# Differential attention on one core: the values as the stationary operand, four query tiles' probabilities moving, the result kept by feature

## The chip, the cores and the metric

The kernel runs on one core of one Trainium2 chip. The metric is the device time of one execution in microseconds. Before the change the median of three runs is 2161.65 us (2161.48 to 2164.58). The engines are TensorE (PE, whose weight loads are listed apart as PEld), VectorE (DVE), ScalarE (ACT), GpSimd (POOL) and SyncE (SP, which here only issues transfers). Each works through its own queue in order.

## The reference, cut to what matters

The program is one decoder layer: three branches (mLSTM, differential attention, cross-attention to a memory) from one normalised input h, merged with sigmoid gates, then an MLP. The change lies in the second branch. It has 8 heads, 1024 positions, query and key width 64 in two copies, and value width 128:

```
s = einsum('bhcqd,bhckd->bhcqk', qblk, kt) * scale      # c = 0, 1
s = where(kpos <= qpos, s, -inf)
p = softmax(s)
a = p[:, :, 0] - lam * p[:, :, 1]
o = einsum('bhqk,bhkv->bhqv', a, vt)
o = rms_norm(o, subln_g) * (1.0 - lam_init)             # over the 128 features of a head
```

Everything is float32. A product of matrices is made of three matmuls: each operand is split into a high part in the reduced format `F32R` and the rest (`split`: a cast on ACT, then a difference on DVE), and the terms high x high, high x low and low x high are summed in PSUM (`mm3`).

## The kernel before, in words

`branch_d` walks over 64 steps `s`, one for each head (`s // 8`) and each tile of 128 queries in it (`i8 = s % 8`). A head is thus two halves of four tiles; `hh` counts the 16 halves. In a step, `scores(s, 0)` and `scores(s, 1)` make the two score tiles (128 queries by up to 1024 keys, in PSUM), mask them and take the row maximum on DVE (L1029), and exponentiate on ACT with the row sum beside it (L1037). `combine(s)` weighs the second copy with lambda and the ratio of the sums and adds it to the first (L1046 to L1050, all on DVE). One step later `turn` transposes the combined probabilities in blocks of 128 by 128 on PE and splits them; two steps later `values` multiplies. There the turned probabilities are the stationary operand, and the values move: one matmul of 256 columns for (high, low) of the values and one of 128 columns for the probabilities' low part, for each block of keys. The two halves of the PSUM tile `po` are scaled by the first sum's reciprocal and added into `doS`, four tiles of queries by 128 features (L1088, L1089). After four steps, `norm` squares and sums over the features (L1098, L1100), takes the power -0.5 on POOL (`rsqrt_mean`, L148 and L149), multiplies (L1104), transposes the four tiles back to features by queries on PE, scales by the subln gain (L1110) and stores the half (`store_y`, L351). The tail of the program reads it much later.

Between these pieces `fill(n)` puts n steps of other matrix work on PE: first the generator `d_gemm`, which projects the query, key and value columns of the next heads (544 steps, the last 32 of them gate steps), then the generator `gates` (three matmuls of 512 columns a step). The gates that `fill` can still draw after those 544 are the 64 steps of the last two groups. While `self.pinned` is true, PE keeps exactly this order. On the other engines and the queue of SP a planner lays out the order when the program is built, and each works in that order.

`wino_gates` comes next: it makes the last gates with seven products for each eight. Its operands with numbers 0 to 2 lie in `hT`; numbers 3 to 6 are loaded from DRAM (`hx<-hc_d`, L1217, one megabyte each), and its weights come as `fr<-in_wgq` (L1188). Its products use, in this order, the operands 0, 2, 4, 5, 6, 3, 1. Its tiles lie in the memory that the tiles of `branch_d` give free: pools are laid one behind another in the order in which they are opened, from the end of the pool of weights `wpg`.

Of the kernel before, what the change touches and what calls it, by code (L numbers as in the profile page):

```python
# [17 lines left out]
P = 128  # L18
D = 1024
# [54 lines left out]
class Layer:  # L74
# [922 lines left out]
    def branch_d(self, pool, sums, gemm, kv, done):  # L997
# [3 lines left out]
        oS, info = {}, {}  # L1001
        gates = self.gates
        NS = 64

# [6 lines left out]
        def scores(s, c):  # L1011
# [4 lines left out]
            if c == 0:  # L1016
                info[s] = [
                    [pool.tile([P, D], F32, tag=f"dpe{q}", name=self.name("dpe")) for q in range(2)],
                    pool.tile([P, 8], F32, tag="dst", name=self.name("dst")),
                ]  # L1020
# [19 lines left out]
            )  # L1040

        def combine(s):
# [4 lines left out]
            V.scalar_tensor_tensor(  # L1047
                out=t8[:, 7:8], in0=t8[:, 7:8], scalar=t8[:, 4:5], in1=self.nlam, op0=ALU.mult, op1=ALU.mult
            )
            V.scalar_tensor_tensor(  # L1050
                out=pe[0][:, 0:n], in0=pe[1][:, 0:n], scalar=t8[:, 7:8], in1=pe[0][:, 0:n], op0=ALU.mult, op1=ALU.add
            )

        def turn(s, h2):

            hf, i = divmod(s % 8, 4)
            if h2 > hf:
                return
            nb = 4 if h2 < hf else i + 1
            pt = self.tp_tile()  # L1060
            for j in range(nb):
                c0 = (h2 * 4 + j) * P
                self.transpose(pt[:, j * P : (j + 1) * P], info[s][0][0][:, c0 : c0 + P])
            aT = pool.tile([P, 2, 512], F32R, tag="daT", name=self.name("daT"))
            self.split(aT[:, 0, 0 : nb * P], aT[:, 1, 0 : nb * P], pt[:, 0 : nb * P])
            info[s].append(aT)

        def values(s):
            hd, i8 = divmod(s, 8)
            hf, i = divmod(i8, 4)  # L1070
            t8 = info[s][1]
            po = self.po_tile()
            first = True
            for h2 in range(hf + 1):
                nb = 4 if h2 < hf else i + 1
                aT = info[s][2 + h2]
                v = kv[hd * 2 + h2][3]
                for j in range(nb):
                    s_ = slice(j * P, (j + 1) * P)
                    last = h2 == hf and j == nb - 1  # L1080
                    self.mm(po[:, 0:256], aT[:, 0, s_], v[j].rearrange("p a d -> p (a d)"), start=first, stop=False)
                    self.mm(po[:, 0:128], aT[:, 1, s_], v[j][:, 0], start=False, stop=last)
                    first = False
            if i == 0:
                oS[s // 4] = pool.tile([P, 4, P], F32, tag="doS", name=self.name("doS"))
            o = oS[s // 4]

            nc.scalar.activation(o[:, i], po[:, 0:128], AF.Copy, scale=t8[:, 6:7])  # L1088
            V.scalar_tensor_tensor(  # L1089
                out=o[:, i], in0=po[:, 128:256], scalar=t8[:, 6:7], in1=o[:, i], op0=ALU.mult, op1=ALU.add  # L1090
            )
            done[0] = s + 1

        def norm(hh, part):
            o = oS[hh]
            if part == 0:
                scr = pool.tile([P, 512], F32, tag="dscr2", name=self.name("dscr2"))
                nc.scalar.activation(scr, o.rearrange("p a d -> p (a d)"), AF.Square)  # L1098
                so = pool.tile([P, 4], F32, tag="dso", name=self.name("dso"))
                V.tensor_reduce(so, scr.rearrange("p (a d) -> p a d", a=4), axis=AX.X, op=ALU.add)  # L1100
                self.rsqrt_mean(so, so, 128, 4)
                info["so"] = so
            if part == 1:
                V.tensor_mul(o, o, info["so"].unsqueeze(2).broadcast_to([P, 4, P]))  # L1104
            if part == 2:
                pt = self.tp_tile()
                for i in range(4):
                    self.transpose(pt[:, i * P : (i + 1) * P], o[:, i])
                y = pool.tile([P, 512], F32, tag="y", name=self.name("yd"))
                nc.scalar.activation(y, pt, AF.Copy, scale=self.gsub)  # L1110
                self.store_y(1, hh // 2, hh % 2, y)
# [5 lines left out]
        for s in range(NS + 4):  # L1117
            hh, i = divmod(s - 2, 4)
            if s < NS:
                scores(s, 0)  # L1120
                fill(3)
            if 2 <= s < NS + 2:
                values(s - 2)
                if i == 3:
                    norm(hh, 0)
            fill(2 if s < NS else 6)
            if s >= 6 and i == 2:
                norm(hh - 1, 2)
            if s < NS:
                scores(s, 1)  # L1130
                fill(1)
            if s >= 6 and i == 1:
                norm(hh - 1, 1)
            if 1 <= s < NS + 1:
# [3 lines left out]
                if s == NS:  # L1138
                    fill(6)
# [829 lines left out]
```

## Time and profile before

| what | value |
|---|---|
| median of three runs | 2161.65 us |
| the profiled execution's own time | 2161.13 us |
| its span | 2159.3 us |
| granted TensorE clock | 1.00 |
| differential attention, first to last score | about 606 to 1080 us |
| its last values, last transposes | to 1097.7 and at 1112.6 us |
| last gates (`wino_gates`) | from 1113 us |

A row of a group of instructions gives line, engine, operation, written tile and read tiles, shapes and count; then busy time in all and mean nanoseconds of one; then the engine's idle time just before them and what ended it. The line L95 is that of the helper `mm`, L98 of `transpose`, L121 and L123 of `split`. The chain of waits lists pieces of the chain that ended last with start, length and count. Ends of matmuls are modelled, so their durations overlap; the spacing of their starts doesn't.

### The profile page before, as it was taken

Reading aid. Unit: us, or ns where it says so; the run is one execution under the profiler, and the core shown is the slowest. Engines: PE = TensorE matmul, PEld = TensorE weight load, DVE = VectorE, ACT = ScalarE, POOL = GpSimd, SP = SyncE. Lnnn points to the kernel's source line nnn. Section 1 sums busy time; section 2 is a strip of 40 time slices with the busy share of each in tenths; the row PEclk is TensorE's granted clock in tenths of the full one; section 3 lists DMA queues with packets and bytes.
Section 4 is the critical chain, followed back from the end, with each engine's and each line's share of the span. In section 5 each row is a group of like instructions: output and inputs, shape, how many; then the busy total and the mean of one; then the engine's idle time right before and its main releaser. Section 6 shows DMA issues by size and latency. Waiting matters only on the chain.

```text
span 2159.3 us, 30669 instructions
## 1 busy us (share of the span) xinstructions
PE 2133.7 (99%) x11049; PEld 1849.6 (86%) x11049; DVE 1421.0 (66%) x2688; ACT 987.2 (46%) x1991; POOL 578.5 (27%) x736
## 2 busy tenths in 40 slices
PE   7999999999999999999999999999999999999999
PEld 5888888898899999999878888888888888888887
DVE  6644475574548877777565433553688889876698
ACT  6543354454346666666554320223534544643331
POOL 2100000000111111111031003202756578565562
PEclk9999999999999999999999999999999999999999
DMA  6115122131433333333253643435434544844443
GB/s 240 46 61 171 39 86 75 41 93 47 171 89 94 98 98 84 92 84 83 79 175 132 237 157 109 147 97 195 160 131 153 201 151 156 295 169 151 156 161 107
DMA packets 134557, 275.95 MB, mean 128 GB/s; under 512 B 13025, under 2 KB 29702, under 8 KB 132358
## 3 DMA queue, kind: packets, MB, share of 16 engines
q1 hardware_dynamic: 128070, 254.07, 36.8%
q10 hardware_dynamic: 6336, 19.93, 2.4%
q8 instruction: 87, 1.43, 0.3%
q14 instruction: 64, 0.52, 0.1%
HBM read 177.45 MB, written 71.34 MB: 115 GB/s over the span
## 4 chain that ended last, share of the span: by engine, by line
PE 92%; DVE 2%; DMA 2%; ACT 1%; issue 0%; POOL 0%; SPq 0%; DVEq 0%; ACTq 0%; POOLq 0%
PE mm L95 52%; PE p L95 27%; PE sc L95 6%; PE po L95 3%; PE tp L98 3%; PE pr L98 1%; DMA hx<-hc_d 0%; PE tp L95 0%; DVE acc L69 0%; DVE w L123 0%; DMA ngb<-g_dng 0%; PE sc L98 0%; DMA wib<-g_dwi 0%; DVE u L69 0%; DMA raw<-in_wd 0%
## 5 line engine op out<-in xcount | busy, mean ns | idle before, releaser
L95 PE MATMUL mm<-w,hT 128*128 128x384 f32 (+3 forms) x2496 | 468.9, 331 | 0.9 <-DVE dsg L126 0.9
L95 PE MATMUL mm<-hT,w 128*128 128x512 f32 x1680 | 408.2, 394 | 0.6 <-ACT gt L500 0.6
L95 PEld LDWEIGHTS mm<-w,hT 128*128 128x128 f32 x2496 | 388.8, 189 | 11.0 <-DVE dsg L126 1.1
L95 PEld LDWEIGHTS mm<-hT,w 128*128 128x128 f32 x1680 | 308.3, 188 | 60.8 <-ACT gt L500 1.2
L95 PE MATMUL p<-xo,wo 128*128 128x512 f32 x1344 | 306.2, 390 | 0.4 <-DVE u L69 0.3
L95 PE MATMUL p<-xd,wo 128*128 128x512 f32 x1344 | 305.0, 390 | 0.0
L95 PEld LDWEIGHTS p<-xo,wo 128*128 128x128 f32 x1344 | 252.0, 188 | 53.3 <-DVE u L69 1.2
L95 PEld LDWEIGHTS p<-xd,wo 128*128 128x128 f32 x1344 | 252.3, 188 | 52.5 <-DVE acc L69 0.3
L95 PE MATMUL mm<-kt,w 128*128 128x512 f32 x1152 | 261.3, 390 | 0.0
L95 PEld LDWEIGHTS mm<-kt,w 128*128 128x128 f32 x1152 | 216.4, 188 | 44.8
L114 ACT CAST wo<-wraw 128x896 fp32r<-128x896 f32 x124 | 116.7, 945 | 223.0 <-PE p L95 86.6
L121 ACT CAST w<-raw 128x256 fp32r<-128x256 f32 (+3 forms) x272 | 139.5, 546 | 143.4 <-PE mm L95 123.2
L123 DVE TENSOR_TENSOR w<-raw,w 128x256 fp32r<-128x256 f32 (+3 forms) x272 | 158.3, 606 | 53.0 <-ACT w L121 52.3
L69 DVE TENSOR_TENSOR wo<-wraw,wo 128x896 fp32r<-128x896 f32 x124 | 151.6, 1232 | 46.5 <-ACT wo L114 46.5
L1288 POOL TENSOR_TENSOR wraw<-wraw 128x128 f32<-128x128 f32 x128 | 94.2, 736 | 214.5 <-DMA wraw<-in_wdown 74.6
L1037 ACT ACTIVATE dpe<-sc,dst,drr 128x256 f32<-128x256 f32 (+7 forms) x128 | 106.6, 833 | 96.7 <-DVE dst L1033 95.9
L148 POOL TENSOR_SCALAR hss<-hss 128x4 f32<-128x4 f32 x8 | 4.1, 516 | 408.7 <-ACT mscr L782 408.7
L1029 DVE CUSTOM_DVE_ANT_0 sc<-sc,tmask 128x256 f32<-128x256 f32 (+7 forms) x128 | 97.1, 759 | 13.8 <-PE sc L95 13.1
L1290 POOL TENSOR_TENSOR wraw<-wraw 128x128 f32<-128x128 f32 x128 | 96.7, 756 | 0.0
L95 PE MATMUL sc<-dk,dq 128*128 128x512 f32 (+3 forms) x384 | 92.0, 348 | 0.0
L1289 POOL TENSOR_TENSOR wraw<-wraw 128x128 f32<-128x128 f32 x128 | 90.5, 707 | 0.0
L69 DVE TENSOR_TENSOR acc<-acc,p 128x512 f32<-128x512 f32 x121 | 80.3, 685 | 15.0 <-PE p L95 14.4
(313 smaller groups left out, 3048.7 us busy)
## 6 DMA issues: line engine op xcount, KB each, us to landing
dk<-dsg SPq DMA_DIRECT2D x64, 256.0 KB, 4.3
wraw<-in_wup SPq DMA_DIRECT2D x64, 256.0 KB, 3.0
r_d<-xts SPq DMA_DIRECT2D x16, 1024.0 KB, 4.1
wraw<-in_wdown SPq DMA_DIRECT2D x64, 256.0 KB, 2.9
raw<-in_wd SPq DMA_DIRECT2D x32, 384.0 KB, 3.3
kraw<-y SPq DMA_DIRECT2D x24, 512.0 KB, 5.0
gl<-gates SPq DMA_DIRECT2D x48, 256.0 KB, 2.7
r_d<-rq ACTq DMA_DIRECT2D x16, 768.0 KB, 4.6
```

The source lines that it names most:

```text
L69: return self.tc.keep_in_program_order(f(*a, **k))
L95: self.pin(self.nc.tensor.matmul(out, l, r, start=start, stop=stop))
L98: self.pin(self.nc.tensor.transpose(out, x, self.ident))
L114: self.cast = self.A.copy(hi, src).ins
L121: a = nc.scalar.copy(hi, src)
L123: return a, nc.vector.tensor_sub(lo, src, f32(hi))
L148: g.tensor_scalar(r, ss, 1.0 / width, EPS, op0=ALU.mult, op1=ALU.add)
L1029: V.tensor_tensor_reduce(out=sc[:, 0:n], in0=sc[:, 0:n], in1=self.tmask[:, D - n : D], scale=1.0, scalar=-3.0e38, op0=ALU.add, op1=ALU.max ...
L1037: nc.scalar.activation(pe[c][:, 0:n], sc[:, 0:n], AF.Exp, bias=t8[:, 2 + c : 3 + c], scale=rr[:, i, c : c + 1], accum_out=t8[:, 4 + c : 5 ...
L1288: G.tensor_add(r[:, 4], r[:, 0], r[:, 3])
L1289: G.tensor_sub(r[:, 5], r[:, 4], r[:, 1])
L1290: G.tensor_sub(r[:, 6], r[:, 1], r[:, 0])
```

## The change

The values become the stationary operand, and the turned probabilities of four query tiles, up to 512 columns, move. So `turn(hh, j)` gathers block j of keys from the four query tiles of a half into one PSUM bank, and `values(hh, j)` makes three matmuls into `po`, which now holds features by queries. Key blocks on the diagonal use only the columns of the tiles that see them. The four combined tiles of a half have to stay until the last block is turned, so each has a buffer of its own, `pe0` to `pe7`. The division by the first sum can no longer be done on the result's rows: `combine` multiplies the second copy by its reciprocal and lambda on POOL, and DVE then multiplies the first copy by its own reciprocal and adds.

The result need not be transposed any more. Its sum of squares over the features runs over partitions: `squares` copies `po`, squares it and splits the squares, and `norm` multiplies them by a column of ones into one row of 512 sums. That row goes through DRAM to 128 partitions by 4, through `rsqrt_mean`, back to DRAM, and returns repeated on all partitions; one DVE instruction multiplies gain and root onto the copy.

The loop has slots, two a step: in slot n the block turned in slot n-1 is multiplied and the next one is turned. `T` gives the slot of each turn, `W` that of each norm. One bank `pt` and one bank `po` serve all turns and all values. After the 64 steps ten slots follow with `fill(4)` each, then `fill(8)` and the last norm. Buffers change: weights `w` 13 to 12, `dv` 17 to 16, `draw` 7 to 6, `doS` and `dpe0` go, `drt` and `pe0` to `pe7` come.

```diff
         def combine(s):
 ...
             V.reciprocal(t8[:, 6:8], t8[:, 4:6])
+            G.tensor_scalar(pe[1][:, 0:n], pe[1][:, 0:n], t8[:, 7:8], self.nlam, op0=ALU.mult, op1=ALU.mult)
             V.scalar_tensor_tensor(
-                out=t8[:, 7:8], in0=t8[:, 7:8], scalar=t8[:, 4:5], in1=self.nlam, op0=ALU.mult, op1=ALU.mult
+                out=pe[0][:, 0:n], in0=pe[0][:, 0:n], scalar=t8[:, 6:7], in1=pe[1][:, 0:n], op0=ALU.mult, op1=ALU.add
             )
 ...
+        def turn(hh, j, bank):
+            c = max(0, j - 4 * (hh % 2))
+            for i in range(c, 4):
+                self.transpose(bank[:, i * P : (i + 1) * P], info[hh * 4 + i][0][0][:, j * P : (j + 1) * P])
+            t = pool.tile([P, 2, 512], F32R, tag="daT", name=self.name("daT"))
+            c = slice(c * P, 512)
+            self.split(t[:, 0, c], t[:, 1, c], bank[:, c])
+            aT[hh, j] = t
+        def values(hh, j):
+            v, t = kv[hh // 2 * 2 + j // 4][3][j % 4], aT.pop((hh, j))
+            c = slice(max(0, j - 4 * (hh % 2)) * P, 512)
+            self.mm(po[:, c], v[:, 0], t[:, 0, c], start=j == 0, stop=False)
+            self.mm(po[:, c], v[:, 1], t[:, 0, c], start=False, stop=False)
+            self.mm(po[:, c], v[:, 0], t[:, 1, c], start=False, stop=j == hh % 2 * 4 + 3)
+        def squares(hh):
+            y = pool.tile([P, 512], F32, tag="y", name=self.name("yd"))
+            nc.scalar.copy(y, po)
+            sq = pool.tile([P, 2, 512], F32R, tag="daT", name=self.name("dsq"))
+            x = pool.tile([P, 512], F32, tag="dscr2", name=self.name("dscr2"))
+            nc.scalar.activation(x, po, AF.Square)
+            self.split(sq[:, 0], sq[:, 1], x)
+            Y[hh] = y, sq
+        def norm(hh, bank):
+            y, sq = Y.pop(hh)
+            for i in range(2):
+                self.mm(bank[0:1, :], ones[:, 0:1], sq[:, i], start=i == 0, stop=i == 1)
+            row = pool.tile([P, 512], F32, tag="drt", name=self.name("drow"))
+            nc.scalar.copy(row[0:1], bank[0:1, :])
+            so = pool.tile([P, 4], F32, tag="dso", name=self.name("dso"))
+            rt = pool.tile([P, 512], F32, tag="drt", name=self.name("drt"))
+            four = lambda d: d[hh].rearrange("(p i) -> p i", i=4)
+            Q = nc.sync
+            Q.dma_start(sums_d[hh : hh + 1], row[0:1])
+            Q.dma_start(so, four(sums_d))
+            self.rsqrt_mean(so, so, 128, 4)
+            Q.dma_start(four(root_d), so)
+            Q.dma_start(rt, root_d[hh].partition_broadcast(P))
+            V.scalar_tensor_tensor(out=y, in0=y, scalar=self.gsub, in1=rt, op0=ALU.mult, op1=ALU.mult)
+            self.store_y(1, hh // 2, hh % 2, y)
+        for hh in range(16):
+            for j in range(hh % 2 * 4 + 4):
+                T[8 * hh + 9 + (j if hh % 2 else 2 * j)] = hh, j
+        def slot(n):
+            bank = lambda: pt if n < 2 * NS else self.sc_tile()[:, 0:512]
+            if n - 1 in T:
+                hh, j = T[n - 1]
+                values(hh, j)
+                if j == hh % 2 * 4 + 3:
+                    squares(hh)
+                    W[n + 1] = hh
+            if n in W and W[n] % 2:
+                norm(W[n], bank())
+            if n in T:
+                turn(*T[n], bank())
+            if n in W and W[n] % 2 == 0:
+                norm(W[n], info["sc"][:, 512:] if n < 2 * NS else bank())
 ...
+        for s in range(NS):
+            scores(s, 0)
+            fill(3)
+            slot(2 * s)
+            fill(1)
+            scores(s, 1)
+            fill(3)
+            slot(2 * s + 1)
+            fill(1)
+            combine(s)
+        for n in range(2 * NS, 2 * NS + 10):
+            fill(4)
+            slot(n)
         fill(8)
-        norm(15, 2)
+        norm(15, self.sc_tile()[:, 0:512])
```

More of the change, by code (lines that the diff above doesn't have):

```diff
@@ L1040, in scores @@
             )
+            if c == 1:
+                done[0], info["sc"] = s + 1, sc
         def combine(s):
@@ L1054, in turn @@
[L1054 to L1111, printed above, removed]
+        def turn(hh, j, bank):
[6 more added lines that the diff above has]
+            aT[hh, j] = t
```

55 lines of the change are left out of this document (18 added, 37 removed).

## The prediction

> **What bounds the kernel now.** I read the profile's page, then busy time by stretches, then the chain of waits, then single groups. The page first:
>
> ```profile
> span 2159.3 us, 30669 instructions
> PE 2133.7 (99%) x11049; PEld 1849.6 (86%) x11049; DVE 1421.0 (66%) x2688; ACT 987.2 (46%) x1991; POOL 578.5 (27%) x736
> ...
> PE 92%; DVE 2%; DMA 2%; ACT 1%; issue 0%; POOL 0%; SPq 0%; DVEq 0%; ACTq 0%; POOLq 0%
> ```
>
> TensorE bounds it: 92% of the chain that ends last is PE. The stretches (columns: PE, PEld, DVE, ACT, POOL busy with counts, granted clock, DMA share, GB/s) show differential attention (620 to 1080), its end with the hand-over to the last gates, and those gates:
>
> ```profile
> 620.00:1080.00 460.00, 459.15 (x2902) 438.18 (x2901) 351.63 (x1028) 284.74 (x713) 64.63 (x60) 1.00 0.35 90
> 1080.00:1130.00 50.00, 47.68 (x233) 39.17 (x232) 31.50 (x50) 26.48 (x52) 16.26 (x21) 1.00 0.56 184
> 1130.00:1240.00 110.00, 110.00 (x485) 90.76 (x484) 57.55 (x86) 41.72 (x68) 11.49 (x15) 1.00 0.52 180
> ```
>
> In the body PE lacks 0.85 us of 460 and DVE has 24% left, so there a saved microsecond of matmul is a saved microsecond. In the 50 us of the hand-over PE is idle 2.3 us already: that place is thin.
>
> **What a matmul really costs.** The busy durations of matmuls overlap, so I price by the chain of waits (start, length, count):
>
> ```profile
> 836.80 1.56 PE mm L95 x9
> 838.36 1.33 PE po L95 x12
> 843.20 0.33 PE tp L98 x3
> 1091.34 0.44 PE tp L98 x4
> 1091.78 4.13 PE mm L95 x18
> 1095.91 1.79 PE po L95 x16
> 343.50 1.08 PE sc L95 x9
> ```
>
> 384 columns cost 1.56/9 = 0.173 us, 512 columns (the gates' mm) 4.13/18 = 0.229, 258 columns (the sc at 343.50) 0.120, and a transpose of 128 columns 0.110. A po pair, 256 and then 128 columns, costs 1.33/6 = 0.222 or 1.79/8 = 0.224: 0.103 for the narrow one, nearly twice its share of 0.120. A stationary block of 128 columns thus has a floor of about 0.11.
>
> The Trainium skill (TensorE: Matmul & The Clock Gate, LDWEIGHTS) puts a weight load at columns / 1.2 ns, 107 ns for 128: the trace agrees. Its rule in Back-to-back issue gap, columns / 2.4 + 2.5 ns, would leave a narrow matmul at 56 ns and speaks against this change; the sum by it stands among the rivals, and the trace disagrees with it.
>
> **The change on PE.** Counts and shapes now:
>
> ```profile
> L95 PE MATMUL po<-dv,daT 128*128 128x256 f32 x288 | 69.5, 321 | 0.0
> L95 PE MATMUL po<-dv,daT 128*128 128x128 f32 x288 | 64.1, 223 | 0.1
> L98 PE MATMUL tp<-ident,dpe 128*128 128x128 f32 x288 | 47.0, 272 | 0.0
> L98 PE MATMUL tp<-ident,doS 128*128 128x128 f32 x64 | 9.6, 272 | 0.0
> ```
>
> Removed: 288 pairs x 0.223 = 64.2, and the 64 transposes of the result x 0.110 = 7.0. Added: per head the even half has value steps of 512, 384, 256 and 128 columns, the odd half five of 512 and then 384, 256, 128; with three matmuls each that is 18 x 0.229 + 6 x 0.173 + 6 x 0.120 + 6 x 0.110 = 6.54 us, x 8 heads = 52.3. The sum over features by the column of ones: 16 x 2 matmuls of 512 columns = 32 x 0.229 = 7.3. The 288 transposes of probabilities stay. Net 52.3 + 7.3 - 64.2 - 7.0 = **-11.6 us**; with 0.222 to 0.224 per pair, -11.3 to -11.9.
>
> **The other engines in the body.** Per half of a head (16 of them), from these rows:
>
> ```profile
> L1047 DVE SCALAR_TENSOR_TENSOR dst<-dst,dv 128x1 f32<-128x1 f32 x64 | 13.9, 217 | 1.2
> L1089 DVE SCALAR_TENSOR_TENSOR doS<-po,dst,doS 128x128 f32<-128x128 f32 x64 | 22.4, 350 | 45.5 <-ACT doS L1088 45.5
> L1100 DVE TENSOR_REDUCE dso<-dscr 128x4 f32<-128x512 f32 x16 | 11.0, 684 | 7.0 <-ACT dscr L1098 7.0
> L1104 DVE TENSOR_TENSOR doS<-doS,dso 128x512 f32<-128x512 f32 x16 | 11.5, 721 | 6.6 <-POOL dso L149 6.6
> L123 DVE TENSOR_TENSOR dsg<-pr,dsg 128x512 fp32r<-128x512 f32 x16 | 11.0, 688 | 2.3 <-ACT dsg L121 2.2
> L1050 DVE SCALAR_TENSOR_TENSOR dpe<-dpe,dst,dpe 128x512 f32<-128x512 f32 x8 | 6.0, 750 | 0.2
> L1098 ACT ACTIVATE dscr<-doS 128x512 f32<-128x512 f32 x16 | 10.1, 632 | 6.7 <-DVE doS L1089 6.7
> L121 ACT CAST daT<-tp 128x512 fp32r<-128x512 f32 x48 | 27.5, 586 | 18.0 <-PE tp L98 17.5 <-PE mm L95 0.4
> ```
>
> DVE loses 4 x (0.217 + 0.350) + 0.684 + 0.721 = 3.67 and gains one split (0.69) and one product (0.75), so it falls by 2.2 x 16 = 36 of 352 us. ACT trades four evictions, a square and the scaled copy for a copy, a square, a cast and the row's copy: about even. Neither gates PE, so I credit nothing.
>
> New is a POOL instruction in every combine: DVE's product now waits for it. No row has its shape; the nearest ones:
>
> ```profile
> L1871 POOL MEMSET tmask<- 128x1024 f32 x1 | 0.9, 949 | 0.0
> L1162 POOL TENSOR_TENSOR hb<-hb,hb 128x512 f32<-128x512 f32 x4 | 6.0, 1502 | 20.2 <-DVE hb L1161 8.8 <-DVE hb L1157 7.4 <-PE tp L98 4.0
> L149 POOL TENSOR_TENSOR drr<-drr,mhalf 128x16 f32<-128x16 f32 x16 | 46.4, 2901 | 1.3
> SPq L351 <- ACT yd L1110: 77.7, 7, 11.3
> ```
>
> With no tensor read, 1024 columns take 0.95; with two, 3.0 (twice the 512 row). Over the mean width of 576 that is 0.53 to 1.7 us, 64 times. Queued on DVE behind the waiting product are the next mask-and-maximum and the splits of turned probabilities, for which PE waits one slot later. But a tile is now first turned two slots, a whole step of some 7 us, after its second scores at the earliest, and were DVE to stand for all of 64 x 1.7 = 109 us, 352 - 36 + 109 = 425 of the remaining 449 us still fit. POOL's 2.9 us power can delay 16 of the 64. I take 1 us of PE stalls, bounds 0 and 6. The norm's relay through DRAM (four dependent transfers on SP per half) blocks the loads behind it; SP stands as long in this trace (up to 11.3 us for the y store) with PE at 99.8%, and the y it makes is read only in the tail: nothing. The smaller rings (w 12, draw 6, dv 16) release their slot before it is asked for again: nothing either.
>
> **The end.** Here I expect the loss.
>
> ```profile
> 1097.55 15.21 PE L95 MATMUL mm<-hT,w 128*128 128x512 f32 x66
> 1112.60 0.60 PE L98 MATMUL tp<-ident,doS 128*128 128x128 f32 x4
> 1116.55 3.06 PE L95 MATMUL mm<-hT,w 128*128 128x512 f32 x12 [0.60 <-ACT gt L500]
> 1129.46 3.06 PE L95 MATMUL mm<-hx,w 128*128 128x512 f32 x12 [1.58 <-DVE u L1248]
> 1079.44 0.99 SPq L1217 DMA_DIRECT2D hx<-hc_d  x2
> 1085.01 1.05 ACT L121 CAST hx<-hx 128x1024 fp32r<-128x1024 f32 x1 [1.61 <-DMA hx<-hc_d]
> 1086.09 1.23 DVE L123 TENSOR_TENSOR hx<-hx 128x1024 fp32r<-128x1024 f32 x1 [0.85 <-ACT hx L121]
> 1087.56 1.05 ACT L121 CAST hx<-hx 128x1024 fp32r<-128x1024 f32 x1 [0.30 <-DMA hx<-hc_d]
> SPq L351 <- ACT yd L1110: 10.2, 1, 10.2
> ```
>
> Now 66 gate matmuls, 15.2 us, stand between the last value matmul and the last transposes; they hide the norm and the loads of the next operands. The fills are 544 of the projection's steps and then 64 gate steps. The new loop has spent 572 when scores end and asks for 4 before each of ten tail slots: 36 are left, so slots 128 to 136 get theirs, and slot 137 and the closing fill(8) get nothing. PE then waits three times, in program order. (1) For the split of the last turned tile: 0.27 transpose, 0.27 and 0.28 for cast and difference of 128 columns, hand-overs: 1.0 us. (2) For copy, square, cast and difference before the ones: 0.59 + 0.63 + 0.59 + 0.69 and 0.3 of hand-overs = 2.8. (3) For operand 4 of the gates. Behind their common base the new pools lie as 6 + 8 + 18 KB, then three daT buffers of 4; the gates' as 4 + 16 + 16 KB and then operand 4, at 36 to 52 KB, on the second and third daT. With 4 + 96 + 16 tiles in that ring the last squares sit in the second, so the load starts after the ones matmuls. Two such loads asked for together at 1079.44 were cast from 1085.01 and 1087.56: 5.6 and 8.1 us; with 1.05, 1.23 and 0.3 that is 8.2 to 10.7, against 24 matmuls of cover, 5.5. So 2.7 to 5.2; I take 3.5, near the undisturbed load. Together 7.3, less the 2.3 idle there now: **+5.0**; bounds +1.5 (no third wait) and +12 (two more casts ahead in ACT, a late load).
>
> **Sum.** -11.6 + 1 + 5.0 = -5.6 us. The profiled execution took 2161.1 (its span of 2159.3 and 1.8 around it), 0.5 below the median of 2161.65: 2155.5 by it, 2156.1 by the median. I say **2156**.
>
> **Rivals.**
> A hidden end: the planner gets the operands loaded early and other work covers the norm. The end costs +1.5 or less and the body 0 to 1: 2150. For it: fr2 now lies on buffers that are free early. Against: nothing is left on PE between.
> Stalls in the body: POOL's product at 3.0 us for deep tiles, behind the 2.9 us power, eats what is left, 64 x 0.08 = 5 us more: 2161. For it: DVE's in-order queue. Against: the 24% that DVE has free.
> The relay ahead of the load (slower): SP issues in order, and the 10.2 us stand behind a y store shows what it does to the gates' loads. If the last norm's first three transfers and the power stand ahead of operand 4, three hops of 2.4 to 3.5 and 1.2 us make the third wait 8 to 12 longer: 2161.1 - 11.6 + 1 + 5 + 11 = 2167. It decides from about two hops.
> Narrow matmuls at their streaming rate alone (slower): with 0.060 for 128 columns, half of 0.120, the values go from 288 x 0.180 = 51.8 to 49.9, the transposes removed are worth 3.8 and the ones cost 7.3: +1.6, and with the body's 1 and the end's 5 it is 2169. Sixteen po matmuls in 1.79 us deny it, where 8 x 0.18 would be 1.44.
>
> The Trainium skill's gap rule is this last rival: by its 216, 162, 109 and 56 ns the sum is 46.8 + 6.9 - 47.6 - 3.6.
>
> **Chances.** Forecast (2152 to 2160) 0.46, hidden end 0.19, body stalls 0.16, relay 0.15, streaming rate 0.04. About 0.2%, 4.3 us, is what can be told from no change: faster is below 2157.3, that is two thirds of the forecast and the hidden end, 0.50; slower is above 2166, most of the relay and the last, 0.16; the same 0.34. The range, 2149 to 2167, leaves out the last case and half of the relay's upper part.
>
> **What would show it.** The three value forms at about 0.23, 0.17 and 0.12 us in the chain and PE at 99.5% or more in the body show the first term; PE idle there with DVE named as releaser, and DVE waiting for POOL in combine, the second. In the last 30 us before the gates PE should stand near 1, 2.8 and 3.5 us, released by the split, by the squares' split and by hx. A body that isn't some 11 us shorter makes the prediction wrong, and so does an end without idle PE.

## The result and the profile after

The changed kernel takes 2230.31 us (median of 4 runs, 2228.8 to 2231.61) beside 2161.57 us for the kernel before on the same chip: a ratio of 1.0315, interval 1.0299 to 1.033. It is 68.7 us slower, where 2156 us and at most 2167 us were predicted. The profiled execution took 2229.75 us, its span 2228.0.

First the page of the changed kernel: its span, the busy time of the engines, and the shares of the chain that ended last.

```profile
span 2228.0 us, 29966 instructions
PE 2142.7 (96%) x10729; PEld 1830.1 (82%) x10729; DVE 1392.3 (62%) x2561; ACT 974.8 (44%) x1959; POOL 647.8 (29%) x800
...
PE 45%; DMA 6%; DVE 5%; POOL 4%; issue 4%; ACT 3%; SPq 1%; ACTq 0%; DVEq 0%; POOLq 0%
```

TensorE (PE) has dropped from 99% of the span to 96%, and from 92% of the chain to 45%. The rest of the chain runs through the other engines and through DMAs: the kernel is no longer bound by its matmuls alone. The count of matmuls is as the change says, 11049 - 576 - 64 + 288 + 32 = 10729.

Next, busy time by stretches (columns as in the prediction: PE, PEld, DVE, ACT, POOL, clock, DMA share, GB/s), first after, then the same end stretch before.

```profile
620.00:1080.00 460.00, 423.54 (x2410) 385.80 (x2409) 303.12 (x847) 248.42 (x634) 120.93 (x115) 0.99 0.36 93
1080.00:1210.00 130.00, 105.50 (x471) 84.65 (x470) 63.87 (x119) 56.63 (x114) 29.00 (x35) 0.92 0.36 110
```

```profile
1080.00:1210.00 130.00, 127.68 (x585) 105.07 (x584) 78.67 (x123) 64.12 (x117) 27.75 (x35) 1.00 0.54 185
```

In the body PE now lacks 36.5 us of 460 where it lacked 0.85; in the 130 us of the end it lacks 24.5 us where it lacked 2.3. VectorE (DVE) is busy for 303 us of the body where it was 352, so it is not short of time.

For an account of the whole span I price each matmul by its columns (0.4167 ns a column and 14 ns, at least 110 ns; this fits the prediction's 0.110, 0.173 and 0.229) and call excess what lies between the starts of two consecutive matmuls above that price. Over the span the priced work falls from 2122.8 to 2108.8 us, by 14.0, and the excess rises from 24.8 to 107.6, by 82.8. That is +68.8, the change of the span. Because the stages shift, I divide the excess by stage: the body goes from 600 us to the start of the last score (1079.0 us before, 1118.5 after), the end from there to 1215. In the body the excess rises from 4.2 to 60.4 us, at the end from 3.4 to 26.4, elsewhere by 4. Body and end excess below are meant so.

Who waits for whom between 600 and 1240, by the view of waits (total, times, longest):

```profile
DVE dpe L1059 <- POOL dpe L1058: 48.0, 45, 2.7
POOL dso L148 <- DMA dso<-d_ss: 37.5, 10, 9.6
DVE yd L1107 <- DMA drt<-d_rs: 34.2, 16, 5.0
PE mm L95 <- ACT u L1246: 16.2, 1, 16.2
PE tp L95 <- DVE daT L123: 14.2, 14, 1.8
PE tp L95 <- ACT daT L121: 8.7, 14, 1.4
PE sc L95 <- ACT dpe L1046: 8.0, 7, 1.7
```

The first three are waits of VectorE and GpSimd (POOL), 120 us together, that the kernel before did not have. The last four are PE's own. (The value matmuls are named tp here, since `po` now comes from `tp_tile`.)

Three kinds of stall come back from head to head. (A) The product of a finished half with its root stands in VectorE's queue, waiting for the last hop of the relay through DRAM, and the split of the next turned probabilities stands behind it. From the timeline (start, length, engine, instruction, idle time before it and releaser):

```profile
819.29 0.57 ACT L121 CAST daT<-tp 128x512 fp32r<-128x512 f32 x1
820.55 0.63 PE L95 MATMUL tp<-daT,dv 128*128 128x512 f32 x2
821.56 0.75 DVE L1107 SCALAR_TENSOR_TENSOR yd<-yd,dv,drt 128x512 f32<-128x512 f32 x1 [2.97 <-DMA drt<-d_rs]
822.23 0.68 DVE L123 TENSOR_TENSOR daT<-tp,daT 128x512 fp32r<-128x512 f32 x1
822.97 0.50 PE L95 MATMUL tp<-daT,dv 128*128 128x512 f32 x1 [1.80 <-DVE daT L123]
```

ACT had cast that tile by 819.86; VectorE stood 2.97 us for `drt`, then took the product and the split, and PE stood 1.80 us ahead of the third value matmul. (B) The combine. VectorE waits for GpSimd's scale, and GpSimd, in this instance, for the relay's sums:

```profile
813.78 0.17 DVE L1057 RECIPROCAL dst<-dst 128x2 f32<-128x2 f32 x1 [0.78 <-ACT dpe L1046]
814.31 0.20 POOL L148 TENSOR_SCALAR dso<-dso 128x4 f32<-128x4 f32 x1 [3.97 <-DMA dso<-d_ss]
814.59 1.01 POOL L149 TENSOR_TENSOR dso<-dso,mhalf 128x4 f32<-128x4 f32 x1
815.60 0.55 POOL L1058 TENSOR_SCALAR dpe<-dpe,dst,dv 128x256 f32<-128x256 f32 x1
816.18 0.49 DVE L1059 SCALAR_TENSOR_TENSOR dpe<-dpe,dst,dpe 128x256 f32<-128x256 f32 x1 [2.24 <-POOL dpe L1058]
```

The scale, 0.55 us of work, starts 1.65 us after its factor was ready at 813.95. (C) The ones matmuls of the even halves wait for ACT's exponential, because they write into the upper bank of the score tile whose lower columns ACT is reading: 8.0 us in 7 waits above.

At the end the predicted three waits are all there:

```profile
1156.86 0.65 PE L95 MATMUL tp<-daT,dv 128*128 128x128 f32 x3 [0.47 <-ACT daT L121]
1159.97 0.40 PE L95 MATMUL sc<-dsq,dso 128*1 128x512 f32 x1 [2.46 <-ACT dsq L121]
1160.70 0.40 PE L95 MATMUL sc<-dsq,dso 128*1 128x512 f32 x1 [0.33 <-DVE dsq L123]
1161.91 0.25 SPq L1102 DMA_DIRECT2D d_ss<-drow  x1
1165.99 0.34 SPq L1103 DMA_DIRECT2D dso<-d_ss  x1
1169.60 1.88 POOL L149 TENSOR_TENSOR dso<-dso,mhalf 128x4 f32<-128x4 f32 x1
1171.51 0.34 SPq L1105 DMA_DIRECT2D d_rs<-dso  x1
1172.92 0.34 SPq L1106 DMA_DIRECT2D drt<-d_rs  x1
1173.31 0.43 SPq L1222 DMA_DIRECT2D hx<-hc_d  x1
1181.90 1.99 ACT L121 CAST hx<-hx 128x1024 fp32r<-128x1024 f32 x2 [10.00 <-DMA hx<-hc_d]
1184.43 2.08 PE L95 MATMUL mm<-hx,w 128*128 128x512 f32 x4 [16.24 <-ACT u L1246]
```

The first is 0.47 us, the second 2.46 + 0.33, the third 16.24: the last load of the gates' operands (L1222) is issued only at 1173.31, behind the four transfers of the last norm on SyncE's queue and the root on GpSimd between them. From its issue to its cast on ACT it takes 8.6 us more.

### The profile page after: what moved, and what is told of

Its sections match the earlier page's. It is cut to its first block, busy times and chain, and to the rows that moved or that the text cites. A ratio compares the mean times of both kernels' runs of the same rounds, so it can differ in the third digit from the quotient of the medians.

```text
span 2228.0 us, 29966 instructions
## 1 busy us (share of the span) xinstructions
PE 2142.7 (96%) x10729; PEld 1830.1 (82%) x10729; DVE 1392.3 (62%) x2561; ACT 974.8 (44%) x1959; POOL 647.8 (29%) x800
## 4 chain that ended last, share of the span: by engine, by line
PE 45%; DMA 6%; DVE 5%; POOL 4%; issue 4%; ACT 3%; SPq 1%; ACTq 0%; DVEq 0%; POOLq 0%
PE p L95 22%; PE mm L95 21%; DMA drt<-d_rs 2%; ACT dpe L1046 1%; POOL dpe L1058 1%; DMA dso<-d_ss 1%; POOL dso L149 1%; PE tp L95 1%; DVE dpe L1059 1%; POOL drr L149 1%; DMA wraw<-in_wdown 1%; DMA d_rs<-dso 1%; DVE u L69 1%; DVE sc L1038 0%; PE sc L95 0%
## 5 line engine op out<-in xcount | busy, mean ns | idle before, releaser
L95 PE MATMUL mm<-w,hT 128*128 128x384 f32 (+3 forms) x2496 | 459.8, 330 | 2.2 <-DVE dst L1042 1.6
L95 PEld LDWEIGHTS mm<-w,hT 128*128 128x128 f32 x2496 | 394.3, 190 | 15.0 <-issue 2.9
L95 PEld LDWEIGHTS p<-xd,wo 128*128 128x128 f32 x1344 | 251.7, 188 | 56.2 <-DVE c L69 1.9
L1058 POOL TENSOR_SCALAR dpe<-dpe,dst,dv 128x128 f32<-128x128 f32 (+3 forms) x64 | 56.8, 888 | 286.0 <-DVE dst L1057 249.5
L95 PE MATMUL tp<-daT,dv 128*128 128x512 f32 (+3 forms) x288 | 74.9, 357 | 23.1 <-DVE daT L123 14.2
```

The lines of the kernel that those rows point to most:

```text
L95: self.pin(self.nc.tensor.matmul(out, l, r, start=start, stop=stop))
L1058: G.tensor_scalar(pe[1][:, 0:n], pe[1][:, 0:n], t8[:, 7:8], self.nlam, op0=ALU.mult, op1=ALU.mult)
```

## Experiments

All times stand beside runs of the kernel before on the same chip. Its medians lay between 2162.6 and 2164.1, so I compare ratios to it; 0.001 is 2.2 us. The changed kernel has 1.0315.

### Taking the suspects away

e1_no_relay: the relay goes, and the root with it.

```
-            (so, rt, four DMAs, rsqrt_mean)
-            V.scalar_tensor_tensor(out=y, in0=y, scalar=self.gsub, in1=rt, ...)
+            V.scalar_tensor_tensor(out=y, in0=y, scalar=self.gsub, in1=y, ...)
```

> Leaves out the root of the norm: the row of sums is made and copied out as before, but its four transfers through DRAM and the two POOL instructions go, and the last product multiplies the copy by the gain and by itself. Theory 'relay': the DVE product that waits for the returning row (34 us of standing in the changed kernel, 16 times) and the POOL pair that waits for the row's sums (37 us, with combine's scaling behind it) hold up the splits that PE waits for, and the last operand load of the gates is queued on SP behind the last relay. Then some 20 to 30 us go in the body and 11 to 14 at the end: 2230 becomes 2187 to 2200, and DVE has no row that waits for a transfer of the norm. Theory 'POOL': combine's scaling on POOL is what holds DVE up; then only the end moves, 2216 to 2220, and PE in the body still lacks some 35 us of 460.

e2_scale_on_dve: the combine's scale moves.

```
-            G.tensor_scalar(pe[1][:, 0:n], ...)
+            V.tensor_scalar(pe[1][:, 0:n], ...)
```

> Same computation; combine's scaling of the second copy moves from POOL to DVE, so that DVE waits for no other engine between the row sums and the combined tile. Theory 'POOL': DVE stood 48 us in 45 waits for that instruction, most of it in front of work PE waits for; without it 2195 to 2208. Theory 'relay': DVE only exchanges a wait for work of 0.3 to 1.1 us each, 64 times; 2222 to 2232.

e3_neither has both edits.

> Both of the last two edits; leaves out the root of the norm. If relay and POOL together make the body's stalls, PE in the body lacks no more than 10 us of what it lacked 36 of, the end keeps a wait for the last squares and a short one for the operand, and the time is 2160 to 2172. If the order of the slots itself (one PSUM bank for all turns, the ones matmuls one slot after the squares) makes them, it stays above 2180.

e4_tail_cover: two filling products instead of four between the tail's slots, which keeps more of them for the end.

```
-            fill(4)
+            fill(2)
             slot(n)
```

> Same computation; only the ten tail slots draw 2 instead of 4 gate steps each, so 16 of the 64 gate steps, 11 us of matmuls, are left to run behind the last values and the last norm. If PE's 16 us wait before the first product with a loaded operand comes from having nothing to do while the relay and the load run, it falls by 9 to 11, less 2 to 4 for thinner tail slots: 2221 to 2226. If the slots in the tail are bound by their splits, it is given back there: 2228 to 2232.

Measured: e1 2203.48 us (1.0186, 1.0171 to 1.0201), e2 2203.37 (1.0187, 1.017 to 1.0204), e3 2192.47 (1.0138, 1.0123 to 1.0153), e4 2225.44 (1.0286, 1.0271 to 1.0301). The body of each, e1, e2, e3:

```profile
620.00:1080.00 460.00, 426.65 (x2442) 392.48 (x2441) 310.26 (x860) 257.02 (x644) 104.14 (x94) 0.99 0.34 88
```

```profile
620.00:1080.00 460.00, 441.89 (x2534) 405.37 (x2533) 349.73 (x950) 265.61 (x668) 69.34 (x62) 1.00 0.38 98
```

```profile
620.00:1080.00 460.00, 436.87 (x2494) 404.49 (x2493) 344.85 (x939) 264.07 (x660) 49.97 (x34) 0.98 0.35 90
```

Without the relay the excess falls from 26.4 to 13.0 us at the end and from 60.4 to 49.2 in the body, so e1 lies between its two cases. It also shows that the relay is not what makes VectorE wait for the scale, for that wait is as long without it:

```profile
DVE dpe L1059 <- POOL dpe L1058: 49.0, 47, 2.6
```

With the scale on VectorE (e2, within its first band) the gain lies in the body, 60.4 to 32.5, although VectorE is then busier by 47 us; so it was not VectorE's load that cost. The two gains do not add up: 28 us each and 38 together. e3 is above 2180, as its second case said. What is left in it is the third kind of stall, which has grown:

```profile
PE sc L95 <- ACT dpe L1046: 18.8, 7, 3.0
```

```profile
673.67 0.68 DVE L123 TENSOR_TENSOR dsq<-dscr,dsq 128x512 fp32r<-128x512 f32 x1
675.19 0.46 ACT L1046 ACTIVATE dpe<-sc,dst,drr 128x128 f32<-128x128 f32 x1
675.80 1.01 PE L95 MATMUL sc<-dsq,dso 128*1 128x512 f32 x2 [2.85 <-ACT dpe L1046]
```

The squares were split by 674.35; the ones matmuls started at 675.80, after the exponential of the score tile whose bank they borrow. Seven waits of 2.7 us on the average, in seven of the eight heads. e4's time is within its band, 6 us less, but not by what was expected: the third wait of the end falls from 16.2 to 13.7 us only, by 2.5 instead of 9 to 11. More cover helps little.

### The borrowed bank

e5_late_ones: the even halves' ones matmuls come one slot later, when the tile kept in `info["sc"]` is the one before.

```
-                    W[n + 1] = hh
+                    W[n + 2 - hh % 2] = hh
```

> The changed kernel, but the even halves' ones matmuls are issued one slot later (slot 8hh+18 instead of 8hh+17), so that the score tile whose upper bank they borrow has had its exponential by then. Nothing is left out. Theory (the borrowed bank makes TensorE wait for ACT's exponential of that score tile, and each such wait is followed by a stretch at half clock): the row of TensorE on sc waiting for ACT dpe L1046 (8.0 us in 7 waits in the changed kernel) falls below 1.5 us, and with the half-clock stretches behind them the time falls from 2230 to 2212-2222 us. Rival (the wait only moves: the following score product now waits for the copy of the row out of the borrowed tile): 2226-2232 us.

e6_neither_late is e3 with this edit, e8_dve_late is e2 with it.

> The kernel of e3_neither (no root of the norm and so no relay; the combine's scale on VectorE) with the even halves' ones matmuls one slot later. It leaves out the root: y is multiplied by itself in its place. Theory: e3's 20 us of body loss in 7 waits of 3 us goes, 2192 us becomes 2163-2178 us. Rival (another wait takes its place): 2186 us or more.

> The kernel of e2_scale_on_dve (all of the computation, relay kept, the combine's scale on VectorE) with the even halves' ones matmuls one slot later. Theory: 2203 us becomes 2180-2190 us, what is left above the kernel before lies for the larger part at the end (the late load behind the last relay, 16-20 us). Rival (the wait only moves): 2199-2205 us.

Measured: e5 2214.1 us (1.0232, 1.0217 to 1.0248), e6 2172.6 (1.0038, 1.0023 to 1.0053), e8 2191.15 (1.0124, 1.0107 to 1.0141). In e5 the wait is down to one:

```profile
PE sc L95 <- ACT dpe L1046: 0.8, 1, 0.8
```

One index moved, and 0.0083 (18 us) go. But that index moves the whole norm of the even halves, relay included: VectorE's wait for `drt` falls from 34.2 to 17.8 us too, so e5 alone does not give the bank's price. e6 against e3, where there is no relay, does: PE's 18.8 us of waits are gone and the time is 0.0100 (22 us) less. The borrowed bank is shown by that pair. The half-clock stretches of e5's expectation were fewer than it says: the changed kernel has two in the body (at 823.8 and 1032.0 us), e5 none. e8 lies 1 us above its band, and 25.0 us of its excess lie at the end and 22.5 in the body, the larger part at the end as expected. e6 shows where the design stands without relay, slow scale and borrowed bank, though it leaves out the root: still 0.4% above the kernel before.

### Order or price

Is the relay dear by its length and the scale by GpSimd's speed, or do both cost because of what stands behind them? e17_relay_spread keeps every instruction of the relay and issues the root two slots and the product five slots later.

```
+            if n:
+                L[n + 2], L[n + 5] = root, product
```

> The changed kernel with the relay alone spread out (root two slots behind the ones matmuls, product five slots behind; SyncE's queue throughout, tail unchanged). Nothing is left out. Theory (the relay costs in the body by VectorE's and GpSimd's place in line): VectorE's wait on drt (34.2 us) falls below 12 us, the body gets back 8-15 us, the end stays as it is: 2213-2223 us. Rival (the body's loss is the scale's and the borrowed bank's alone): 2227 us or more.

Measured: 2220.54 us (1.0268, 1.025 to 1.0286), 10 us less, within its band though VectorE's wait for `drt` fell only to 16.0 us, not below 12:

```profile
DVE yd L1111 <- DMA drt<-d_rs: 16.0, 5, 5.3
PE tp L95 <- DVE daT L123: 7.9, 9, 1.2
```

PE's waits for the split fell from 14.2 to 7.9 us, the excess in the body from 60.4 to 52.6, and the end stayed at 26.3. So in the body the relay's place in line costs, with every transfer of it kept. Only half of the theory is borne out: GpSimd's wait for the sums did not fall but rose from 37.5 to 48.0 us, and VectorE's for the scale from 48.0 to 56.2. The gain came by the product's place in VectorE's queue.

e12_blend_later calls VectorE's half of the combine after the next query tile's first score, with the scale left on GpSimd.

```
             scores(s, 0)
+            if s:
+                blend(s - 1)
             fill(3)
```

> The changed kernel, but VectorE's half of the combine (the product and sum of L1059) is issued after the next query tile's first score instead of right behind GpSimd's scale; the scale stays on GpSimd. Nothing is left out or moved to another engine. Theory (it is VectorE's place in line that costs, not where the scale is computed): VectorE's wait for the scale (48.0 us in 45) falls below 8 us and the time from 2230 to 2198-2210 us, as far as it fell with the scale on VectorE. Rival (GpSimd's own 1.7 us for the scale, or the tile being ready later, is what costs): 2222 us or more.

Measured: 2236.61 us (1.034, 1.0325 to 1.0356). The theory seemed to fall, but the view of waits shows why the run does not test it:

```profile
DVE dpe L1064 <- POOL dpe L1058: 47.0, 47, 2.7
```

47.0 us in 47 waits, as before: on VectorE the planner lays out the order, and it put the instruction back. (The 6 us more than in the changed kernel are hardly beyond the noise and stay unexplained.) e13_blend_behind therefore states the order as a constraint.

```
+            self.behind(b.ins, info["top"])       # the next tile's first reduction
+            self.behind(b.ins, info.pop("late"))  # the next split of turned probabilities
```

> The changed kernel with VectorE's half of the combine (the product and sum) held by an order constraint behind the next query tile's first score reduction and the next split of turned probabilities; the scale stays on GpSimd. In e12_blend_later the planner put this instruction back in its old place behind the scale (VectorE's wait 43.5 us in 43), so that run moved nothing. Nothing is left out. Theory (VectorE's place in line): its wait for the scale falls below 15 us and the time from 2230 to 2198-2214 us. Rival (GpSimd's time for the scale itself, or the lateness of the tile that it makes ready): 2222 us or more.

Measured: 2211.34 us (1.0219, 1.0201 to 1.0237).

```profile
DVE dpe L1063 <- POOL dpe L1058: 1.1, 1, 1.1
```

The wait is gone and so are 0.0096 (21 us), with the scale still on GpSimd and nearly as slow (54.6 us busy between 600 and 1240 where it was 56.7). PE's waits for the split of turned probabilities, 14.2 and 8.7 us in the changed kernel, are down to 0.5. It is VectorE's place in line. Moving the scale to VectorE (e2) had brought 28 us, 7 more; here PE waits 6.0 us for the combined tile itself, which is now ready later, where it waited 2.7.

### All of it mended

e7_deferred is e8 with the spread relay, e4's tail, and GpSimd's queue for the last relay.

> The kernel of e8_dve_late with the relay spread out: the root is issued two slots behind the ones matmuls and the product with the root five slots behind them, so that GpSimd and VectorE find their data landed; the last half's relay goes by GpSimd's queue instead of SyncE's, and the tail places two filling products instead of four between its slots. Nothing is left out. Theory (it is the order of the instructions behind the relay, not the relay's length or its traffic): VectorE's wait on drt (34 us) and GpSimd's on dso (37 us) fall below 5 us each ahead of the end, the late load of the end comes within 5 us, and the time is within 6 us of e6_neither_late, 2163-2180 us. Rival (the relay costs by its length or traffic wherever it is placed): no faster than e8_dve_late.

Measured: 2182.68 us (1.0084, 1.0069 to 1.0099), 0.004 better than e8, but 10 us above e6 where 6 were expected: PE still waited 11.7 us for the late load. The relay no longer goes by SyncE's queue, yet the load (L1234 there) stood in that queue for 13.3 us, until the relay's third transfer `d_rs<-dso` had landed, and ACT could cast its data only at 1135.28. The body excess, 20.0 us, is level with e6's 21.6. VectorE's wait for `drt` ahead of the end is 7.5 us, not below 5; GpSimd's for the sums rose to 142.1 us, but there the scale no longer stands behind it.

e9_turned_later calls the transposes of the turned queries and keys two products later.

```
-            return [(3, q_), (5, s_), (10, k_)]
+            return [(5, q_), (7, s_), (12, k_)]
```

> The kernel of e7_deferred, and the transposes of the turned queries and keys are called two products later (steps 5, 7 and 12 of the next token tile instead of 3, 5 and 10). Nothing is left out. In e7_deferred 19 of the 22 stalls of more than 0.25 us in the body stand ahead of these transposes, 13.1 us together, waiting for VectorE's evacuation of the other bank. Theory (VectorE, which now carries the scale, is late by about one product there): these stalls fall below 3 us, 2183 us becomes 2169-2175 us. Rival (VectorE is late by its load, and the wait follows the transposes to their new place or shows up ahead of the scores): 2180 us or more.

Measured: 2183.26 us (1.0089, 1.0072 to 1.0106): no change. The stalls ahead of these transposes went, and 8.0 us came back ahead of the third value matmul; the rival was right.

e10_last_on_pe takes the last half's norm off the relay: the squares as stationary blocks against the column of ones, the root on GpSimd, four transposes of its broadcast columns.

```
-        norm(15, self.sc_tile()[:, 0:512])
+        so = last_sums(self.sc_tile()[:, 0:512])
+        fill(8)
+        last_norm(so, self.sc_tile()[:, 0:512])
```

> The kernel of e9_turned_later, but the last half's norm does without the relay through DRAM: its sums come out query by query (eight small products with the squares as the stationary block), the root is taken on GpSimd and turned into rows by four transposes of its broadcast columns, eight filling products later. Nothing is left out. Theory (the 12 us at the end is the relay of norm 15 by way of the loads and splits queued behind it): the wait ahead of the first product of the last gate stage falls from 12 to 0-3 us, and the time is 8-12 us below e9_turned_later, 2158-2167 us. Rival (that load is late by its own transfers, not by the relay): within 3 us of e9_turned_later.

Measured: 2168.55 us (1.0024, 1.0014 to 1.0033), 14 us less than e9: more than the 8 to 12 expected, though 1.5 us above the band. The third wait of the end is down from 11.3 to 3.0 us, and the end (its stretch of the windows) is near that of the kernel before:

```profile
PE mm L95 <- ACT u L1277: 3.0, 1, 3.0
```

```profile
1080.00:1210.00 130.00, 125.04 (x566) 101.41 (x565) 76.55 (x123) 65.72 (x122) 26.72 (x33) 1.00 0.49 165
```

So the relay of the last norm is what held up the gates' operands.

Then the same with the scale on each engine. e11_pool_blend_later is e10 with the scale on GpSimd and e12's call, e14_all_behind the same with e13's constraint, e15_scale_on_act is e10 with the scale on ACT, e16_scale_mixed is e14 with the scale of each head's last query tile on VectorE, and that tile's blend no longer held behind the next split.

> The kernel of e10_last_on_pe with the scale back on GpSimd and VectorE's half of the combine issued after the next query tile's first score. Nothing is left out. Theory (what is left in e10_last_on_pe is VectorE late by its load, 354 us busy of 460 in the body, with 7 stalls of 1.1 us ahead of the values): the stalls go with the 44 us that VectorE gets back, 2168 us becomes 2156-2164 us, no slower than the kernel before. Rival (GpSimd, which now does the scale and the roots, makes the roots late): 2168-2180 us.

> The kernel of e11_pool_blend_later with the same order constraint as e13_blend_behind. Nothing is left out. Theory (place in line): 2192 us becomes 2160-2175 us. Rival (GpSimd's scale is late however VectorE is placed): 2185 us or more.

> The kernel of e10_last_on_pe with the combine's scale on ACT (its factor made by a small product on VectorE ahead of it) instead of VectorE. ACT is busy for 272 us of 460 in the body, VectorE for 354. Nothing is left out. Theory (what is left in e10_last_on_pe is VectorE's load): 2168 us becomes 2156-2165 us. Rival (VectorE stands behind ACT as it did behind GpSimd): 2172 us or more.

> The kernel of e14_all_behind with the scale of the last query tile of each head (1024 columns, the tile whose turning waits for it soonest: 6 stalls of 0.9 us in e14) on VectorE, the others on GpSimd. Nothing is left out. Theory: 5 us less than e14, 2160-2166 us, level with the kernel before. Rival (the stall moves to the next wait): 2167-2170 us.

Measured: e11 2192.21 us (1.0132, 1.0115 to 1.0149), e14 2168.23 (1.0025, 1.0015 to 1.0035), e15 2174.88 (1.0054, 1.0037 to 1.0071), e16 2167.49 (1.0018, 1.0008 to 1.0029). The wait of VectorE for the scale, in e11 and e14:

```profile
DVE dpe L1064 <- POOL dpe L1058: 51.9, 51, 2.5
```

```profile
DVE dpe L1063 <- POOL dpe L1058: 6.3, 7, 1.1
```

e11 lies above both its cases because the planner again put the call's instruction back; e14, with the constraint, is in its band. The two differ in that constraint and the place of the call: 45.6 us of waits and 0.0107 (23 us) of time, the second demonstration that it is order. The expectation of e11 and e15, that e10's rest was VectorE's load, fell: e14, with 23 us less on VectorE in the body, is level with e10, and e15, with 26 us less, is 6 us slower, as its rival said. e16 can't be told from e14, as its rival said too.

Of the four repairs three were measured alone on the changed kernel, 18 (e5), 10 (e17) and 21 us (e13), and one on top of others, 14 us (e10 against e9). With e4's tail and e9's later transposes e14 has them all and is 63 us below the changed kernel. That the four add up to 63 too is in part chance: e4's 6 us are not among them, and e1, e2 and e3 showed that such gains do not add. What stays open is the last 4 to 5 us: e14 still has an excess of 15.7 us in the body and 9.2 at the end, 17 more than the kernel before, more than the 14.0 or 11.6 that the matmuls save. No version here beats the kernel before.

## Why the prediction was wrong

**The matmuls: right.** The prediction's first term was -11.6 us, -14.0 by the price used above; the difference is the old pair, measured at 0.223 us and priced here at 0.231. The chain of waits after shows the three value matmuls of 512 columns at the price forecast, 3 x 0.229 = 0.69:

```profile
1010.63 0.69 PE tp L95 x3
```

From start to start the value matmuls of 512, 384, 256 and 128 columns take 0.231, 0.173, 0.117 and 0.111 us (medians of this trace). The rival of the streaming rate is out: it needs 0.060 for 128 columns. The gap rule that stands behind that rival in the prediction was read too widely: the section of the Trainium skill that it names (TensorE: Matmul & The Clock Gate, Back-to-back issue gap) gives the rule for an isolated matmul and says that it counts too little for a stream of narrow ones.

**The body: wrong, and the step that decides.** It said 1 us of PE stalls with bounds 0 and 6, and the body's excess grew by 56. Two sentences of that step failed.

The first reads that were VectorE to stand for all of 109 us, 425 of the remaining 449 us would still fit. This counts capacity. PE waits one slot after its transposes for the split of that very tile, so standing at that moment costs PE nearly as much however idle VectorE is on the average (2.97 us of standing and 1.80 of PE in the rows under (A)): VectorE waited 48.0 us for the scale, and its busy time in the body fell to 303 us, and still the stalls came. The step had named the splits as queued behind the waiting product and then weighed them by the sum. The price of the scale was inside its bounds, 0.53 to 1.7 us at the mean width; measured (shape, count, busy, mean):

```profile
L1058 POOL TENSOR_SCALAR dpe<-dpe,dst,dv 128x1024 f32<-128x1024 f32 x8 | 13.7, 1709 | 47.5 <-DVE dst L1042 35.9 <-DVE dst L1057 11.6
L1058 POOL TENSOR_SCALAR dpe<-dpe,dst,dv 128x512 f32<-128x512 f32 x8 | 6.1, 768 | 42.6 <-DVE dst L1057 42.6
```

so 0.77 us for 512 columns and 1.71 for 1024, 0.89 on the average of all 64. Nor was it what GpSimd has ahead of the scale: without the relay's sums VectorE waited as long (49.0 us in e1), though they lengthen single waits, as under (B). What failed is the weighing by the sum alone. e13 shows the order at 21 us. "Stalls in the body" among the rivals had the mechanism (VectorE's in-order queue) but sized it by load again, at 5 us.

The second is "nothing" for the norm's relay. It looked at SyncE's queue alone, and in the body it held there: none of PE's stalls names a load. But the relay has two more instructions in other queues, the root on GpSimd and the product on VectorE, and each stands until its hop has landed. e17 shows 10 us for the product's place; the root's is not shown apart.

A third cause was on no list. Where the even halves' sums are put is in the code, `info["sc"][:, 512:]`, and the wait counts the whole tile, not the bank. It cost 22 us in e3, where PE waited 18.8 us for it (e6 against e3); in the changed kernel, where PE waited 8.0, it is a part of e5's 18 us that was not measured apart. The prediction counted the ones matmuls' columns and never asked what they wait for outside the tail.

**The end: two waits of three near, the third wrong.** Forecast were 1.0, 2.8 and 3.5 us; measured were 0.47, 2.79 and 16.24. The third is the rival "the relay ahead of the load", which had said 8 to 12 us longer; it was 12.7. The step had the load start right behind the ones matmuls, because operand 4's buffer comes free then; it was issued 12 us later, in SyncE's order behind the relay. The hops were 4.1 us from `d_ss` to the next issue, 2.9 for `dso` to land, 2.5 for GpSimd's two instructions and 1.4 for `d_rs`. Given 15%, it was what happened; added to the body's 56 it is part of a time that no case held. e10 shows it at 14 us. Of the end's 26.4 us of excess 19.5 are the three waits, 1.6 an earlier wait of this kind (the ones of half 14, at 1129.28), some 2 the half clock behind the long wait; the rest is small gaps.

**The sum.** In place of -11.6 + 1 + 5.0 stand, in the span, -14.0 for the matmuls, +56 for the body, +23 for the end, and 4 elsewhere. (At -11.6 for the matmuls the excess would be 2 less.)

## What to carry to other kernels

An engine's idle share says nothing of a wait put into its queue: name the instruction behind it, and ask by when somebody needs that one. A chain that crosses engines and DRAM should be cut where it waits, each later piece issued when its data has landed; but where a planner lays out the order, moving a call can do nothing, as in e12, and the order has to be stated. And a change that saves a half per cent of the bound engine must not add a wait of 2 us per period to anything that feeds it.

## What the runs showed of the chip

After some stalls PE ran at half clock. In the body of e13 this happened seven times, in seven of the eight heads; the windows around the first, and the longer of PE's two stalls ahead of it (the other, at 672.42, was 0.68 us):

```profile
670.00:675.70 5.70, 3.30 (x21) 2.61 (x20) 5.37 (x12) 4.58 (x12) 2.59 (x3) 1.00 0.56 177
675.80:679.20 3.40, 3.40 (x14) 3.40 (x13) 1.97 (x8) 1.34 (x3) 1.93 (x2) 0.51 0.66 174
679.30:685.00 5.70, 5.70 (x37) 5.30 (x36) 2.63 (x9) 2.93 (x8) 1.77 (x3) 1.00 0.27 58
```

```profile
674.47 0.63 PE L95 MATMUL sc<-dsq,dso 128*1 128x512 f32 x2 [1.72 <-ACT dpe L1046]
```

The granted clock is 1.00, then 0.51 for the 3.4 us in which PE's work is dense again, then 1.00. The records give these stretches a length of 3.413 us or whole multiples of it: 10.24 in e7, 17.07 in the changed kernel, where the stretch begins at 1171.9 us, 3.7 us into PE's long wait, and outlasts the wait by 4.6. The Trainium skill (TensorE: Matmul & The Clock Gate, What's actually happening) has the half rate begin after an idle window of about 3.4 us, and its window of 3413 ns agrees with the lengths. The trigger doesn't agree: here no single stall was longer than 1.72 us, and PE was busy for 3.30 of the 5.70 us before. Nor does the length of a stall decide: the body of the changed kernel has 18 stalls of 1.06 to 1.80 us and two such stretches.

What decides can be worked out from the traces. In each trace all stretches start on one grid of steps of 3.413 us (to 3 ns). I laid that grid over 600 to 1215 us of all 19 traces and took the steps at full clock. In the 57 that were followed by half clock PE was idle for 49 to 100% of the step; in the 3252 others it was idle for at most 54%. So it is the idle share of a step of this fixed grid, with the limit near a half, and the stalls of a step add up: 0.68 and 1.72 us in the step ahead of the stretch above, 53% of it. Where a border of the grid divides stalls of that length, they can leave the clock alone. A step at half clock doubles what the matmuls in it cost, up to 1.7 us on top of the stall.

Small hops through DRAM were long for 2 KB: 1.1 to 4.5 us from one issue to the next in the changed kernel (`d_ss` to `dso`, `d_rs` to `drt`), 11 us from the row's store to the issue of the last broadcast at the end (1161.91 to 1172.92, GpSimd's 2.5 us among them). GpSimd's two instructions for a root of 4 columns took 0.5 and 1.9 us there, 0.20 and 1.01 at 814.31, and 0.22 and 1.36 on the average of the 16.
